# V turned by VectorE instead of TensorE, and seven Strassen products summed in PSUM, in a decoder block on one core

## The chip, the cores and the metric

The kernel runs on one core of a Trainium2 chip. A core has five engines with instruction queues of their own, each served in order: TensorE (PE in the profile, with its weight loads as PEld), VectorE (DVE), ScalarE (ACT), GpSimd (POOL) and SyncE (SP), which issues most of the DMAs. TensorE writes to PSUM, eight banks of 128x512 float32; the other tiles lie in SBUF, and the large intermediates in DRAM. The metric is the device time of one execution in microseconds. Lower is better.

## The reference, cut to what matters

The block has sequence 2048 and width 1024, all in float32. One input projection gives 72 tiles of 128 columns; the tiles are numbered f = 0 to 71 below.

```python
proj = x @ w_in + b_in                        # (2048, 1024) @ (1024, 9216)
q, k, v, g_attn, u_lru, g_lru, gate_logits = split(proj)   # 12, 12, 12, 4, 8, 8, 16 tiles of 128
q, k = rope(q), rope(k)
o_g, lse_g = dilated_band_attention(q_g, k_g, v_g)         # 3 groups of 8 heads, bands of 128 keys
attn = sum_g softmax(lse)_g * o_g
y_a = (attn * silu(g_attn)) @ w_attn_proj
u = causal_depthwise_conv(u_lru);  h = rg_lru(u)           # a scan over positions
y_b = (h * silu(g_lru)) @ w_lru_proj
merged = sigmoid(gate_a) * y_a + sigmoid(gate_b) * y_b
out = layer_norm(alpha * x + merged @ w_out + b_out)
```

V enters the result only through a sum that is linear in it, and that sum is multiplied by silu(g_attn): if a tile of V and the tile of silu(g_attn) beside it both change their sign, nothing changes.

## The kernel before, in words

**Stages.** Stage A computes the input projection with everything that follows it per column tile (rotary, the recurrence, the gates); stage B is the attention; then come the projections of the two branches and the output layer. The change lies in stage A. There the result is held with features on partitions and 512 tokens along the free axis, so that a tile of the projection is 128 features by 512 tokens. The attention wants V with tokens on partitions, so V has to be turned.

**Products.** Every matrix product takes three matmuls of 128x512 per 128 rows of the contraction: each operand is split in a high part (`h`, the rounded copy that ScalarE makes) and a rest (`l`, the difference that VectorE makes), and high times high, high times rest and rest times high are summed. A product of one 128-column tile with half the contraction (512 rows) and 512 tokens is thus 12 matmuls into one PSUM bank.

**Quads.** `plan` lists 72 quads: 36 pairs of column tiles (f0, f1) for the first 1024 tokens, then the same 36 for the second. A quad has four results: two tiles by two token chunks (c0, c1). The first quad of each half is computed plainly with eight products. All others use the Strassen-Winograd scheme with seven products, numbered 1 to 7; `UNIT` names the combination of weights of each (A11, A12, S1 to S4, A22), `BLK` that of x (B11, B21, B22, T1 to T4). The x side is prepared once per half, the weight side for each quad: a weight tile is loaded or summed (S), copied by ScalarE (`h`) and subtracted by VectorE (`l`). For the second half the rests are loaded from DRAM.

**After a product.** The order of the products within a quad is MID (1, 6, 7, 5, 2, 4, 3) for nearly all quads. Each product has a bank of its own from a pool `q` of four, and `evacuate` takes each bank out: ScalarE copies product 1 to SBUF (`e`), VectorE adds product 6 to it (`u`), product 7 to that (`v`), product 5 to `u` again, and four further VectorE instructions (`result`, through `total`) add the last product of each result and its bias. That is seven VectorE instructions and one ScalarE copy for a quad. The results of odd tiles (f1) come out negated. Each result starts a chain (`qk_chain`, `v_chain`, `silu_chain`, `mg_chain`, `lru`): a Python generator whose steps are released by the planner.

**V before.** `v_chain` has TensorE turn the 128x512 result with four transposes (`vtp<-ident,y`, L358) into a bank from a pool `t` of two; ScalarE copies the bank to SBUF (`vs`, L366) and takes the sign back; SyncE stores `vs` to `v_scr` (L370) in pieces of 128 features of a token. There are 12 V tiles and four chunks, so 48 of these.

**What sets the order.** The instruction order of every engine is written out by hand: the main loop runs over `where`, one entry (a tick) per product. In each tick it issues the product, then the events due in this tick (weight loads, copies, splits), then the steps of the chains, then `evacuate`. A chain's step runs when its lag in ticks is over, when its tiles are free, and when the planner's budget of each engine it names (2.75 us per tick, minus what was spent) is not used up; the costs in the `Ask` calls are the planner's. Tiles that a DMA stores are given back two ticks after the issue (`give_sent`); their next writer waits for the DMA to land.

Of the kernel before, what the change touches and what calls it, by code (L numbers as in the profile page):

```python
# [31 lines left out]
def hybrid_block_kernel(ctx: ExitStack, tc: tile.TileContext, a: dict, out: bass.AP):  # L32
# [89 lines left out]
    MID, EDGE, FIRST = (1, 6, 7, 5, 2, 4, 3), (1, 2, 6, 7, 4, 5, 3), (1, 2, 3, 6, 7, 5, 4)  # L122
# [89 lines left out]
    def hi_lo(n, kk, src, eng=dve):  # L212

        t = XB[n][:, kk]
        act.activation(t[:, 0], src, AF.Copy)  # L215
        eng.tensor_tensor(out=t[:, 1], in0=src, in1=flat(t[:, 0]), op=ALU.subtract)
# [47 lines left out]
    def prep_w(s, j):  # L264
# [5 lines left out]
        spend(ACT=.66)  # L270
        if (s, j // 2) not in LO:
            LO[s, j // 2] = take_lo(f"l{j}_{s}")
        l = LO[s, j // 2][1][:, j % 2]
        if plan[s][2] is None or not plan[s][0]:
            tt(dve, l, r, flat(h), ALU.subtract)
            spend(DVE=.71)
        give(r)
        U[s, n] = (h, l)
# [69 lines left out]
    vs_free = [sl_p.tile([P, 4, P], F32, name=f"vs{j}") for j in range(2)]  # L348
    tog = {"n": 0}

    def v_chain(vt, sgn, f, c):
        g, hp = divmod(f - FT_V, 4)
        st = {}

        def turn():
            tp = st["tp"] = ps.tile([P, 4, P], F32, tag="t", name=f"vtp{f}_{c}", bufs=2)
            for b in range(4):
                pe.transpose(tp[:, b, :], flat(vt)[:, b * P:(b + 1) * P], ident)  # L358
# [7 lines left out]
        act.activation(vs, st["tp"], AF.Copy, scale=sgn)  # L366
# [3 lines left out]
        sp.dma_start(dst.rearrange("(b p) f -> p b f", p=P), vs)  # L370
        vs_free.append(vs)
# [26 lines left out]
    def silu_chain(y, sgn, f, c):  # L398
# [3 lines left out]
        act.activation(y, y, AF.Identity, scale=0.25 * sgn, bias=bq[:, f:f + 1])  # L402
# [153 lines left out]
    for h in range(2):  # L556
        for p, (kind, f0, f1) in enumerate(seq):
            plan.append((h, ((f0, kind), (f1, kind)), None if p == 0 else EDGE if p == len(seq) - 1 else FIRST if p == 1 else MID, p, kind))
    NQ = len(plan)
    ticks = [8 if pl[2] is None else 7 for pl in plan]  # L560
    base = [sum(ticks[:s]) for s in range(NQ + 1)]
# [45 lines left out]
    def product(s, j):  # L607
# [4 lines left out]
        else:  # L612
            n, x, first, last, end = UNIT[order[j]], XB[BLK[order[j]]], True, True, True
        if first:
            Q["b"] = ps.tile([P, CH], F32, tag="q", name=f"q{j}_{s}", bufs=4)
        bank = Q["b"]
        h, l = U[s, n]
        i = 0
        for kk in range(4):
            ks = slice(kk * P, (kk + 1) * P)  # L620
            for w, xx in ((h, 0), (h, 1), (l, 0)):
                pe.matmul(bank, w[:, ks], x[:, kk, xx], start=(first and i == 0), stop=(last and i == 11))  # L622
                i += 1
            if i == 6:
                run(pe_late)
        if end:
            del U[s, n]
            give(h)
            u = units_of(s).index(n)
# [3 lines left out]
    def evacuate(s, j):  # L633
        half, _, order, _, _ = plan[s]
        b = Q["b"]
        c0, c1 = 2 * half, 2 * half + 1
        if order is None:
            fi, k, c = PLAIN[j]
            if k:
                result(s, fi, c0 + c, b, None)  # L640
            return
        pid = order[j]
        if pid == 1:
            Q["e"] = take(f"e{s}", F32)
            act.activation(Q["e"], b, AF.Copy)
        elif pid == 2:
            result(s, 0, c0, b, Q["e"])
        elif pid == 6:
            Q["u2"] = take(f"u{s}", F32)
            tt(dve, Q["u2"], Q["e"], b, ALU.subtract)  # L650
        elif pid == 7:
            Q["u3"] = take(f"v{s}", F32)
            tt(dve, Q["u3"], Q["u2"], b, ALU.add)
        elif pid == 5:
            result(s, 1, c1, b, Q["u3"])
# [936 lines left out]
```

## Time and profile before

| | us |
|---|---|
| median of three runs | 2104.55 (2104.39 to 2104.73) |
| span of the profiled execution | 2101.9 |
| TensorE busy in the span | 2086.3 (99%) |
| VectorE busy | 1662.7 (79%) |
| ScalarE busy | 1116.7 (53%) |
| GpSimd busy | 493.1 (23%) |

The span is the time from the first to the last instruction of the profiled execution; the timed runs take some microseconds more than a span. Stage A is the stretch from the start to 1443.7 us, the attention that to about 1643 us. "Busy" of TensorE is the union of its matmuls, which overlap: a matmul listed with 390 ns starts its successor much earlier. What a matmul costs is therefore read from the distances between starts.

### The profile page before, as it was taken

The numbers are of one execution on the slowest core, as the hardware profiler recorded it, in microseconds if no ns is written. First come the engines' busy times: TensorE is split into PE (matmuls) and PEld (weight loads), VectorE is DVE, ScalarE is ACT, GpSimd is POOL, SyncE is SP. The second block draws the span as 40 slices with busy tenths as digits, with TensorE's granted clock in tenths as the row PEclk, the third lists the DMA queues.
The fourth block names the chain that finished last, engine by engine and source line by source line (L and its number), as shares of the span: only waits on it lengthen the run. The fifth ranks groups of instructions, "written<-read, shape, count | busy, mean of one in ns | idle before, by whom it ended". The sixth has DMA issues, their size and how long they took to land.

```text
span 2101.9 us, 35814 instructions
## 1 busy us (share of the span) xinstructions
PE 2086.3 (99%) x12016; PEld 1726.9 (82%) x12016; DVE 1662.7 (79%) x3179; ACT 1116.7 (53%) x2341; POOL 493.1 (23%) x468
## 2 busy tenths in 40 slices
PE   8999999999999999999999999999999999999998
PEld 7888888888888888888888888888999888888887
DVE  8987888889988867787877888877999645576667
ACT  6455456457457565666666775766999411211100
POOL 1111111110111011231221222222545344431120
PEclk9999999999999999999999999999999999999999
DMA  8987997987997967777779778769996788864432
GB/s 271 276 261 225 274 285 216 282 283 235 278 294 242 332 208 204 231 227 220 225 254 278 254 252 266 252 219 374 355 359 236 228 296 281 298 224 160 154 105 71
DMA packets 327160, 524.69 MB, mean 250 GB/s; under 512 B 105536, under 2 KB 135232, under 8 KB 323136
## 3 DMA queue, kind: packets, MB, share of 16 engines
q1 hardware_dynamic: 307088, 489.54, 70.5%
q0 software_dynamic: 12256, 19.42, 5.5%
q10 hardware_dynamic: 7632, 13.44, 1.7%
q8 instruction: 96, 1.57, 0.3%
q14 instruction: 88, 0.72, 0.1%
HBM read 317.14 MB, written 190.45 MB: 241 GB/s over the span
## 4 chain that ended last, share of the span: by engine, by line
PE 91%; DVE 3%; DMA 3%; ACT 2%; issue 1%; SPq 0%; DVEq 0%; ACTq 0%
PE q L622 66%; PE yb L1340 3%; PE yb L1341 3%; PE z L1451 3%; PE yb L1342 3%; PE z L1450 3%; PE z L1452 3%; ACT p L1023 2%; DVE p L1015 2%; PE ya L1419 1%; PE ya L1418 1%; PE ya L1420 1%; PE g L492 1%; PE vtp L358 1%; DMA B<-k_scr 1%; DMA o_scr<-ot 1%
## 5 line engine op out<-in xcount | busy, mean ns | idle before, releaser
L622 PE MATMUL q<-xT,hS 128*128 128x512 f32 x1680 | 521.0, 391 | 0.0
L622 PE MATMUL q<-xT,l 128*128 128x512 f32 x1120 | 436.0, 389 | 0.0
L622 PE MATMUL q<-xB,hA 128*128 128x512 f32 x1248 | 388.9, 393 | 6.0 <-ACT xB L215 6.0
L622 PEld LDWEIGHTS q<-xT,hS 128*128 128x128 f32 x1680 | 312.9, 188 | 69.0 <-issue 5.5
L622 PE MATMUL q<-xB,l 128*128 128x512 f32 x904 | 352.9, 390 | 0.0
L622 PEld LDWEIGHTS q<-xB,hA 128*128 128x128 f32 x1248 | 233.8, 189 | 57.3 <-ACT xB L215 6.0
L622 PEld LDWEIGHTS q<-xT,l 128*128 128x128 f32 x1120 | 210.2, 188 | 44.1
L622 PEld LDWEIGHTS q<-xB,l 128*128 128x128 f32 x904 | 170.3, 188 | 36.0
L245 POOL DMA_DIRECT2D wS<-in_w_in_dram x70 | 61.9, 950 | 491.5 <-DMA wS<-in_w_in_dram 140.0
L622 PE MATMUL q<-xB,hS 128*128 128x512 f32 x560 | 174.0, 392 | 0.0
L1023 ACT ACTIVATE p<-p,sta 128x256 f32<-128x256 f32 (+1 forms) x384 | 172.7, 469 | 1.2 <-PE pt L1034 0.8
L622 PE MATMUL q<-xT,hA 128*128 128x512 f32 x560 | 173.0, 390 | 0.0
L269 ACT ACTIVATE hA<-wA 128x512 fp32r<-128x512 f32 x218 | 134.9, 623 | 54.4 <-DMA wA<-in_w_in_dram 24.9
L269 ACT ACTIVATE hS<-S 128x512 fp32r<-128x512 f32 x175 | 109.0, 623 | 79.3 <-DVE S L227 49.0
L227 POOL TENSOR_TENSOR S<-S,wA 128x512 f32<-128x512 f32 x35 | 45.5, 1301 | 391.8 <-DVE S L227 208.8
L622 PEld LDWEIGHTS q<-xT,hA 128*128 128x128 f32 x560 | 104.7, 188 | 23.0 <-issue 1.5
L622 PEld LDWEIGHTS q<-xB,hS 128*128 128x128 f32 x560 | 104.0, 188 | 22.4 <-issue 1.5
L1015 DVE CUSTOM_DVE_ANT_0 p<-s,mask 128x256 f32<-128x256 f32 (+1 forms) x384 | 116.4, 360 | 0.2 <-PE s L1008 0.2
L1451 PE MATMUL z<-wo,mh 128*128 128x512 f32 (+1 forms) x264 | 101.0, 383 | 0.0
L1452 PE MATMUL z<-wo,ml 128*128 128x512 f32 (+1 forms) x264 | 101.0, 383 | 0.0
L1450 PE MATMUL z<-wo,mh 128*128 128x512 f32 (+1 forms) x264 | 101.0, 383 | 0.0
L227 DVE TENSOR_TENSOR l<-wA,hA 128x512 fp32r<-128x512 f32 x113 | 79.3, 702 | 26.9 <-ACT hA L269 26.6
(204 smaller groups left out, 4257.0 us busy)
## 6 DMA issues: line engine op xcount, KB each, us to landing
wA<-in_w_in_dram SPq DMA_DIRECT2D x253, 256.0 KB, 4.7
wl_scr<-l SPq DMA_DIRECT2D x105, 512.0 KB, 5.2
l<-wl_scr SPq DMA_DIRECT2D x105, 512.0 KB, 4.6
sw<-y SPq DMA_DIRECT2D x384, 64.0 KB, 3.2
wS<-in_w_in_dram SPq DMA_DIRECT2D x70, 256.0 KB, 4.8
wS<-in_w_in_dram POOLq DMA_DIRECT2D x70, 256.0 KB, 6.3
qh_scr<-hi SPq DMA_DIRECT2D x48, 256.0 KB, 5.5
v_scr<-vs SPq DMA_DIRECT2D x48, 256.0 KB, 4.4
```

Of the source, the lines that this page charges most:

```text
L227: eng.tensor_tensor(out=out, in0=in0, in1=in1, op=op)
L245: pool.dma_start(t, w_part(s, x), accum_op=ALU.add)
L269: act.activation(h, r, AF.Copy)
L622: pe.matmul(bank, w[:, ks], x[:, kk, xx], start=(first and i == 0), stop=(last and i == 11))
L1015: dve.tensor_tensor_reduce(out=st["p", i, j][:, h, lo:256], in0=st["s", i, j // 2][h][:, j % 2, lo:256], in1=mask[:, lo:256], scale=1.0, s ...
L1023: act.activation(p, p, AF.Exp, scale=-1.0, bias=s[:, h:h + 1], accum_out=s[:, 2 + h:3 + h])
L1340: pe.matmul(yb, WL[f][:, 0, k], xx[:, 0], start=(k == 0), stop=False)
L1341: pe.matmul(yb, WL[f][:, 0, k], xx[:, 1], start=False, stop=False)
L1342: pe.matmul(yb, WL[f][:, 1, k], xx[:, 0], start=False, stop=(k == 7))
L1450: pe.matmul(z, mh[:, k], w[:, 0, hs], start=(k == 0), stop=False)
L1451: pe.matmul(z, mh[:, k], w[:, 1, hs], start=False, stop=False)
L1452: pe.matmul(z, ml[:, k], w[:, 0, hs], start=False, stop=(k == 7))
```

## The change

Three things change in stage A, all in the code that issues it.

1. **V.** The four transposes, the ScalarE copy and SyncE's store of each V result go. VectorE turns the result in 32x32 blocks within SBUF (one instruction, `vs<-y`, L359 of the new file): the block in partition group a and token group b holds 32 tokens by 32 features afterwards. Four DMAs, one for each group of 32 partitions, put the blocks at their places in `v_scr`; ScalarE issues them, in runs of 32 features (128 bytes). `v_scr` holds the same layout as before. The sign of the odd V tiles is no longer taken back; instead the odd tiles of silu(g_attn) keep their negative sign, by a negated bias.
2. **Sums in PSUM.** Products 1, 6 and 5 go into one bank (A), one after another without clearing; ScalarE copies the bank after each (`e`, `u`, `v`). Products 7 and 4 go into another (C), product 2 into B and product 3 into D. T2 is made with the opposite sign so that product 6 adds. Each result is then one VectorE instruction: B with `e`, C with `v`, D with `v`, and C (after product 4) with `u`. Pool `q` has six banks, pool `t` is gone.
3. **Order.** The products stand as 1, 2, 7, 6, 3, 5, 4, and product 4 is issued four products into the next quad, after its product 6. In the last quad of a half product 4 comes last. The events of the unit that product 4 uses (A22) move with it.

```diff
+    ORDER, LAST = (1, 2, 7, 6, 3, 5, 4), (1, 2, 7, 6, 5, 3, 4)
+    BANK = {1: "A", 2: "B", 6: "A", 7: "C", 5: "A", 3: "D", 4: "C"}
...
+        if n == "T2":
+            act.activation(t[:, 0], src, AF.Copy, scale=-1.0)
+            dve.scalar_tensor_tensor(out=t[:, 1], in0=src, scalar=-1.0, in1=flat(t[:, 0]), op0=ALU.mult, op1=ALU.subtract)
+            return
...
-            for b in range(4):
-                pe.transpose(tp[:, b, :], flat(vt)[:, b * P:(b + 1) * P], ident)
-            give(vt)
-
-        yield Ask(cond=lambda: tog["n"] < 2)
-        tog["n"] += 1
-        pe_later(2, turn)
-        yield Ask(lag=3, cond=lambda: len(vs_free) > 0, ACT=.66)
-        vs = vs_free.pop(0)
-        act.activation(vs, st["tp"], AF.Copy, scale=sgn)
-        tog["n"] -= 1
-        yield Ask()
-        dst = v_scr[g][hp // 2][c * CH:(c + 1) * CH, (hp % 2) * P:(hp % 2) * P + P]
-        sp.dma_start(dst.rearrange("(b p) f -> p b f", p=P), vs)
-        vs_free.append(vs)
+        yield Ask(need=1, DVE=.72)
+        vs = take(f"vs{f}_{c}", F32)
+        dve.transpose(vs, flat(vt))
+        give(vt)
+        yield Ask(lag=2, ACT=1.4)
+        dst = v_scr[g][hp // 2][c * CH:(c + 1) * CH].rearrange("(b i) f -> i b f", i=32)
+        for a in range(4):
+            f0 = (hp % 2) * P + 32 * a
+            act.dma_start(dst[:, :, f0:f0 + 32], vs[32 * a:32 * a + 32].rearrange("p (b f) -> p b f", f=32))
+        give_sent(vs)
...
+        js = list(range(8 if pl[3] == 0 else 7 if pl[3] == len(seq) - 1 else 6))
+        own = [(s, j) for j in js]
+        where += own[:4] + ([(s - 1, 6)] if pl[3] > 1 else []) + own[4:]
...
+            n, x, last, end = UNIT[order[j]], XB[BLK[order[j]]], True, True
+            first = order[j] in (1, 2, 7, 3)
+        b = s, BANK[order[j]] if order else "P"
         if first:
-            Q["b"] = ps.tile([P, CH], F32, tag="q", name=f"q{j}_{s}", bufs=4)
+            Q[b] = ps.tile([P, CH], F32, tag="q", name=f"q{j}_{s}", bufs=6)
...
+        if pid in (1, 6, 5):
+            n = {1: "e", 6: "u", 5: "v"}[pid]
+            Q[s, n] = take(f"{n}{s}", F32)
+            act.activation(Q[s, n], b, AF.Copy)
         elif pid == 2:
-            result(s, 0, c0, b, Q["e"])
+            result(s, 0, c0, b, Q[s, "e"])
+            give(Q.pop((s, "e")))
-        elif pid == 6:
-            tt(dve, Q["u2"], Q["e"], b, ALU.subtract)
-        elif pid == 7:
-            tt(dve, Q["u3"], Q["u2"], b, ALU.add)
-        elif pid == 5:
-            result(s, 1, c1, b, Q["u3"])
-            tt(dve, Q["u2"], Q["u2"], b, ALU.add)
...
+    def between(s, j):
+        b = order.index(5)
+        if j == b:
+            result(s, 1, 2 * plan[s][0] + 1, Q[s, "C"], Q[s, "v"])
+        if j == max(b, order.index(3)):
+            result(s, 0, 2 * plan[s][0] + 1, Q[s, "D"], Q[s, "v"])
+            give(Q.pop((s, "v")))
...
+        if T:
+            between(*where[T - 1])
```

`between` runs in the tick after product 5, so the results that need `v` are issued one product after the copy.

**TensorE, at a V quad.** The names are q(place in the quad)_(quad): `q0_5` is the bank of product 1 of quad 5. Before, the four transposes of a V result stand in the middle of a product:

```order
L358 MATMUL vtp25_1_1244<-ident_180,y25_1_1181 128x128 x4
L622 MATMUL q6_4_1237<-xB22_365,hS4_4_1153 128x512 x2
L622 MATMUL q6_4_1237<-xB22_365,l6_4_1155 128x512
...
L622 MATMUL q0_5_1265<-xB11_272,hA11_5_1176 128x512 x2
L622 MATMUL q0_5_1265<-xB11_272,l0_5_1178 128x512
...
L358 MATMUL vtp24_0_1272<-ident_180,y24_0_1211 128x128 x4
```

Now no transposes stand there, product 6 goes into product 1's bank (`q0_6`), product 4 of quad 5 into the bank of its product 7 (`q2_5`) in the middle of quad 6, then product 3 (`q4_6`) and product 5, again into `q0_6`:

```order
L625 MATMUL q0_6_1415<-xT2_425,hS2_6_1400 128x512 x2
L625 MATMUL q0_6_1415<-xT2_425,l2_6_1373 128x512
...
L625 MATMUL q2_5_1275<-xT4_582,hA22_5_1396 128x512 x2
L625 MATMUL q2_5_1275<-xT4_582,l6_5_1398 128x512
...
L625 MATMUL q4_6_1556<-xB22_362,hS4_6_1428 128x512 x2
L625 MATMUL q4_6_1556<-xB22_362,l4_6_1430 128x512
...
L625 MATMUL q0_6_1415<-xT1_524,hS1_6_1453 128x512 x2
L625 MATMUL q0_6_1415<-xT1_524,l4_6_1430 128x512
```

So between two products of bank A stand two others, in which ScalarE's copy of the bank has to be done.

**ScalarE, at the V quads 10 and 11.** Before, one copy `e` and the copies `vs` of the turned V stand among the copies of weights (hA, hS):

```order
L335 ACTIVATE hi_1_2277<-y_1_1977 128x512
L269 ACTIVATE hA_10_2301<-wA_10_2107 128x512
L366 ACTIVATE vs_219<-vtp_1_2257 128x512
L645 ACTIVATE e_2314<-q_10_2283 128x512
L269 ACTIVATE hA_10_2329<-wA_10_2212 128x512
L335 ACTIVATE hi_0_2333<-y_0_2055 128x512
L366 ACTIVATE vs_220<-vtp_0_2290 128x512
L269 ACTIVATE hS_10_2360<-S_10_2189 128x512
L269 ACTIVATE hA_11_2392<-wA_11_2271 128x512
L366 ACTIVATE vs_219<-vtp_0_2349 128x512
```

Now `v` and `e` stand there, and the stores in groups of four:

```order
L365 DMA v_scr_77<-vs_0_2301 32x16x32 x4
L342 ACTIVATE hi_0_2352<-y_0_2134 128x512
L274 ACTIVATE hA_10_2371<-wA_10_2263 128x512
L274 ACTIVATE hS_11_2375<-S_11_2265 128x512
L649 ACTIVATE v_2387<-q_10_2195 128x512
L274 ACTIVATE hS_11_2402<-S_11_2290 128x512
L365 DMA v_scr_77<-vs_1_2355 32x16x32 x4
L365 DMA v_scr_77<-vs_1_2357 32x16x32 x4
L649 ACTIVATE e_2424<-q_11_2389 128x512
L274 ACTIVATE hS_11_2439<-wS_11_2123 128x512
L365 DMA v_scr_77<-vs_0_2422 32x16x32 x4
```

Two groups stand back to back right ahead of an `e` here; such a pair stands at eleven places of stage A.

**VectorE, at a V quad.** Before, three sums out of PSUM (`u`, `v`, `u`) stand between the results:

```order
L227 TENSOR_TENSOR u_2547<-e_2520,q_11_2522 128x512
L227 TENSOR_TENSOR l_11_2564<-S_11_2390,hS_11_2562 128x512
L227 TENSOR_TENSOR S_12_2566<-wS_12_2420,wA_12_2475 128x512
L227 TENSOR_TENSOR y_0_2457<-y_0_2457,cos_637 128x512
L227 TENSOR_TENSOR sw_0_2484<-sw_0_2484,sin_638 128x512
L227 TENSOR_TENSOR v_2571<-u_2547,q_11_2549 128x512
L227 TENSOR_TENSOR S_12_2586<-S_12_2566,wA_12_2508 128x512
L227 TENSOR_TENSOR l_12_2590<-wA_12_2475,hA_12_2588 128x512
L568 SCALAR_TENSOR_TENSOR y_1_2593<-q_11_2573,bn,v_2571 128x512
L227 TENSOR_TENSOR u_2547<-u_2547,q_11_2573 128x512
```

Now two results with `v` stand together, and the two turned tiles follow:

```order
L567 SCALAR_TENSOR_TENSOR y_1_1811<-q_7_1669,bn,v_1790 128x512
L567 SCALAR_TENSOR_TENSOR y_1_1813<-q_7_1735,b_193,v_1790 128x512
L232 TENSOR_TENSOR l_8_1807<-wS_8_1548,hS_8_1830 128x512
L232 TENSOR_TENSOR gw_0_1835<-gr_202,gw_0_1835 128x128
L359 STREAM_TRANSPOSE vs_1_1838<-y_1_1811 128x512
L359 STREAM_TRANSPOSE vs_1_1840<-y_1_1813 128x512
```

The three sums are gone from VectorE's queue, and one instruction per V result has come.

More of the change, by code (lines that the diff above doesn't have):

```diff
@@ L270, in prep_w @@
         spend(ACT=.66)
+        U[s, n] = h
+        if plan[s][2] is not None and plan[s][0]:
+            give(r)
+            return
         if (s, j // 2) not in LO:
@@ L612, in product @@
         else:
-            n, x, first, last, end = UNIT[order[j]], XB[BLK[order[j]]], True, True, True
+            n, x, last, end = UNIT[order[j]], XB[BLK[order[j]]], True, True
+            first = order[j] in (1, 2, 7, 3)
+        b = s, BANK[order[j]] if order else "P"
         if first:
-            Q["b"] = ps.tile([P, CH], F32, tag="q", name=f"q{j}_{s}", bufs=4)
-        bank = Q["b"]
-        h, l = U[s, n]
+            Q[b] = ps.tile([P, CH], F32, tag="q", name=f"q{j}_{s}", bufs=6)
+        bank = Q[b]
+        h = U[s, n]
+        u = units_of(s).index(n)
+        l = LO[s, u // 2][1][:, u % 2]
         i = 0
@@ L621, in product @@
             for w, xx in ((h, 0), (h, 1), (l, 0)):
-                pe.matmul(bank, w[:, ks], x[:, kk, xx], start=(first and i == 0), stop=(last and i == 11))
+                pe.matmul(bank, w[:, ks], x[:, kk, xx], start=(first and i == 0), stop=(last and i == 11),
+                          skip_group_check=not first and order is not None)
                 i += 1
@@ L628, in product @@
             give(h)
-            u = units_of(s).index(n)
             if u % 2 or u == 6:
@@ L925, in hybrid_block_kernel @@
     low = NS
-    where = [(s, j) for s in range(NQ) for j in range(ticks[s])]
     for T, (s, j) in enumerate(where):
```

68 lines of the change are left out of this document (25 added, 43 removed).

## The prediction

> **What bounds the kernel now.** I read the page first: the span, TensorE's share, its row in forty slices, the granted clock and the chain that ended last.
>
> ```profile
> span 2101.9 us, 35814 instructions
> PE 2086.3 (99%) x12016; PEld 1726.9 (82%) x12016; DVE 1662.7 (79%) x3179; ACT 1116.7 (53%) x2341; POOL 493.1 (23%) x468
> ...
> PE   8999999999999999999999999999999999999998
> ...
> PEclk9999999999999999999999999999999999999999
> ...
> q1 hardware_dynamic: 307088, 489.54, 70.5%
> ...
> PE 91%; DVE 3%; DMA 3%; ACT 2%; issue 1%; SPq 0%; DVEq 0%; ACTq 0%
> ```
>
> TensorE sets the end, at full clock. The change lies in stage A, so next comes the table by stretches (columns: length, then busy time of PE, PEld, DVE, ACT, POOL, clock, DMA share, GB/s).
>
> ```profile
> 100.00:1100.00 1000.00, 1000.00 (x4529) 817.22 (x4528) 827.74 (x1248) 572.30 (x940) 165.40 (x172) 1.00 0.82 251
> 1100.00:1443.00 343.00, 343.00 (x1526) 278.89 (x1525) 268.05 (x374) 227.15 (x361) 80.50 (x65) 1.00 0.82 261
> ```
>
> In stage A TensorE has no hole at all, while VectorE is at 83% and ScalarE at 57% of the first stretch. So a TensorE instruction that goes is worth its full pitch, a VectorE instruction that goes is worth nothing by itself, and anything that makes TensorE wait costs its full length.
>
> **Term 1, the transposes that go.** All 48 lie in stage A, four to a V result; the timeline of TensorE around one group gives their pitch.
>
> ```profile
> L358 PE MATMUL vtp<-ident,y 128*128 128x128 f32 x192 | 28.5, 272 | 0.0
> ```
>
> ```profile
> 1086.23 0.39 PE L622 MATMUL q<-xB,l 128*128 128x512 f32 x1
> 1086.46 0.60 PE L358 MATMUL vtp<-ident,y 128*128 128x128 f32 x4
> 1086.82 0.71 PE L622 MATMUL q<-xB,hS 128*128 128x512 f32 x2
> 1087.37 0.40 PE L622 MATMUL q<-xB,l 128*128 128x512 f32 x1
> 1087.60 0.62 PE L622 MATMUL q<-xB,hS 128*128 128x512 f32 x2
> 1088.06 0.39 PE L622 MATMUL q<-xB,l 128*128 128x512 f32 x1
> ```
>
> From one `l` matmul to the next, with three matmuls, it is 1088.06 - 1087.37 = 0.69 us; with a group of four transposes between it is 1087.37 - 1086.23 = 1.14 us. So a group costs 0.45 us, and 48 x 0.45 = 21.6 us go. (The busy time of 28.5 us counts overlap and is not what they cost.) The number of 128x512 matmuls stays: seven products of twelve. Summing in PSUM needs no extra one.
>
> **What VectorE gains and pays.** It loses three sums a quad and gets one turn per V result.
>
> ```profile
> L227 DVE TENSOR_TENSOR u<-e,q 128x512 f32<-128x512 f32 x70 | 47.7, 682 | 27.2 <-PE q L622 27.1
> L227 DVE TENSOR_TENSOR v<-u,q 128x512 f32<-128x512 f32 x70 | 47.7, 681 | 25.1 <-PE q L622 25.0
> L227 DVE TENSOR_TENSOR u<-u,q 128x512 f32<-128x512 f32 x70 | 47.4, 676 | 0.0
> L227 DVE TENSOR_TENSOR rp<-y,sw 128x512 f32<-128x512 f32 x64 | 74.3, 1166 | 0.4
> ```
>
> The turn stands in no row. It moves 128x512 float32 like the sums (0.68 us); the dearest row of that size, the regrouping `rp`, has 1.17 us. I take 0.7. Then 47.7 + 47.7 + 47.4 = 143 us leave and 48 x 0.7 = 34 us (at most 56) come. Worth on the path: nothing, since TensorE was not waiting for VectorE. It is cover for what follows.
>
> **What ScalarE pays.** Two more copies out of PSUM in each of 70 quads, 48 copies `vs` fewer, and 192 DMA issues.
>
> ```profile
> L645 ACT ACTIVATE e<-q 128x512 f32<-128x512 f32 x70 | 41.1, 588 | 93.3 <-PE q L622 84.6 <-POOL sw L227 6.4 <-DMA mg_scr<-y 2.2
> L366 ACT ACTIVATE vs<-vtp 128x512 f32<-128x512 f32 x48 | 27.6, 589 | 30.4 <-DMA v_scr<-vs 14.1 <-PE vtp L358 12.4 <-PE q L622 3.9
> ```
>
> Copies: 140 x 0.59 - 48 x 0.59 = +54 us. An issue of 32 partitions in sixteen pieces of 128 bytes is in no row. The nearest ones, by line (minimum, median and maximum in ns), are the old V store, one ScalarE store, the rotary halves (32 partitions each), and a pair of stores with pieces of 128 bytes, `qh` and right behind it `ql`:
>
> ```profile
> L370 SPq DMA_DIRECT2D v_scr<-vs x48: 365/384/1181, 106.6 to 1105.0; - x48
> L386 ACTq DMA_DIRECT2D mg_scr<-y x5: 326/326/327, 1426.3 to 1445.3; - x5
> L307 SPq DMA_DIRECT2D sw<-y x384: 507/588/1542, 61.5 to 1390.1; - x192
> L341 SPq DMA_DIRECT2D qh_scr<-hi x16: 524/577/1058, 77.1 to 1293.7; - x16
> L341 SPq DMA_DIRECT2D ql_scr<-rp x16: 2115/2678/5558, 77.8 to 1294.4; - x16
> 847.31 2.42 SPq L307 DMA_DIRECT2D sw<-y  x4
> ```
>
> A group of four costs ScalarE's queue between 4 x 0.326 = 1.3 us and, if each of the later three waits as `ql` does, 0.58 + 3 x 2.68 = 8.6 us. I take 2.4 us: the last row is four issues of 32 partitions in a row, and `ql` per piece agrees (it waits behind 2048 pieces; a quarter of 2.68 is 0.67, and 0.58 + 3 x 0.67 = 2.6). So 48 x 2.4 = 115 us come, and ScalarE goes from 572 to about 720 us in the first stretch: busy, not full.
>
> **Term 2, ScalarE's copies are now in TensorE's way.** Product 6 may not start before `e` has left bank A, product 5 not before `u`, and the next C not long after `v`. Between stand two products of 4 x 0.68 = 2.72 us, so a copy may end 5.4 us after its product. How late ScalarE is today shows at its worst in the timeline: product 1 ends where product 6 starts (first row), and `e` comes 5.2 us later.
>
> ```profile
> 568.75 0.62 PE L622 MATMUL q<-xT,hS 128*128 128x512 f32 x2
> ...
> 573.97 0.58 ACT L645 ACTIVATE e<-q 128x512 f32<-128x512 f32 x1
> ```
>
> ```profile
> ACT e L645 <- PE q L622: 84.6, 27, 7.2
> ACT hi L335 <- DVE rp L227: 36.3, 14, 8.1
> ```
>
> At 27 of 70 copies ScalarE was early and waited. Late ones come from ScalarE standing behind VectorE (second row, up to 8.1 us), which gets rarer with an emptier VectorE. The eleven pairs of groups are the new strain: the pair stands in the tick of the copied product, so it has three products, 8.2 us, for 2 x 2.42 + 0.59 = 5.4 us, and 2.7 us of lateness fit. If the second group also waits as `ql` does (2.1 us more), 0.6 us fit; say seven of eleven are 2 us late, then 7 x 1.4, about 10 us, are lost. Below, nothing. I take 2.5 us, near the row of four issues.
>
> **Term 3, the first Strassen quad.** Here both engines are late from the start.
>
> ```profile
> 11.48 0.62 PE L622 MATMUL q<-xB,hA 128*128 128x512 f32 x2
> ```
>
> ```profile
> 40.32 2.49 DVE L227 TENSOR_TENSOR xcB<-xcB,xcB 128x512 f32<-128x512 f32 x4
> ```
>
> ```profile
> 41.04 2.44 ACT L215 ACTIVATE xT<-xcB 128x512 fp32r<-128x512 f32 x4 [2.26 <-DVE xcB L227]
> ```
>
> `u` now stands behind these four T4 copies and one weight copy. One more weight sum ahead of the `xcB` differences, and T2's dearer form, move them by about 1 us, so T4 ends at 44.5 and `u` at 45.5. Product 5 is the fourteenth; the second starts at 11.48, so it is due at 11.48 + 12 x 2.72 = 44.1. I book 1.3 us, between 0 and 3. T3, needed two products earlier than today, is still in time.
>
> **Term 4, the end of stage A.** Product 4 is now last and leaves its bank by one VectorE sum (0.68 us); the attention's first scores may want that bank. 0 to 1 us; I take 0.5.
>
> **V's stores.** SyncE loses 48 issues, which nobody waited for. Nobody reads `v_scr` before the end of stage A, but a tile is given back two ticks after the issue. Stores of 128-byte pieces land a little later than the old V stores (L341, then L370):
>
> ```profile
> DMA to landing us min/median/max: 4.2/5.7/11.1
> ```
>
> ```profile
> DMA to landing us min/median/max: 2.3/4.4/7.7
> ```
>
> The 32 stores of L341 go by with TensorE full, so I book nothing. The Trainium skill ("DMA: Bandwidth & Descriptors", Specifications) speaks against the change: it asks for at least 512 bytes, since a smaller transfer is read, modified and written. By the rows here the landing agrees with a loss, of 1.3 us each, off the path; by the rule alone the DMA engines would be the bound, which is the last rival.
>
> **Sum.** 2101.9 - 21.6 + 2.5 + 1.3 + 0.5 = 2084.6 us of span. The timed median lies 2104.55 - 2101.9 = 2.65 us above the span, so **2087 us**.
>
> **Rivals.**
> - *ScalarE is late more often.* For it: 43 of 70 copies `e` were late already, and there are three times as many. Against it: ScalarE keeps a quarter free. With ten waits of 1 us at `u` and `v` and half of the pairs' 10 us, 15 us go: 2104.55 - 21.6 + 1.8 + 15 = 2100 at the edge, typically 2097.
> - *The waits eat the whole gain*, the pairs' 10 us and ten waits of 1 us together: 2104.55 - 21.6 + 1.8 + 20 = 2105, no change.
> - *The issues fill ScalarE* (slower). A V quad and the one behind it last 2 x 19.5 = 39 us; ScalarE's other work there is 2 x 11.2 us (572 us over 51 quads), copies gone and come cancel, so four groups have 16.6 us, 4.15 us each. Beyond that TensorE waits 48 us for each further microsecond; the gain is gone at 4.6 us. At the longest `ql` wait for a whole group, 5.56 us: 48 x 1.41 = 68 us, 2151 us. For it speaks the `ql` row, against it that a group has as many pieces as one `qh`, which goes in 0.58 us.
> - *The DMA engines fill up* (slower). A packet of the SyncE queue takes 0.705 x 16 x 2101.9 / 307088 = 77 ns on average. The V pieces rise from 24576 to 98304. If time goes by packets, 73728 x 77 ns / 16 = 355 us come on a stretch that has 180 us free; if by bytes, none. It decides from 39 ns per packet; at 45 ns it costs 27 us, 2112 us. Against it: L341's landings.
>
> That the transposes stay is no rival: none is left in TensorE's order.
>
> **Chances and range.** The forecast (2080 to 2095) 0.60, the first rival 0.17, no change 0.09, ScalarE full 0.10, DMA full 0.04. A measurement of this kernel can tell about 0.2% (4.2 us) from no change. Faster is forecast and first rival, 0.77; same 0.09; slower 0.14. The range, 2079 to 2106, takes in the first rival and no change, leaves out the slower ones, and below allows the transposes' pitch and no stall at all.
>
> **What would show it.** Right: stage A ends near 1426 us with TensorE's busy time equal to its length; `e`, `u`, `v` show as releasers of TensorE with a few microseconds in all; a group of stores takes about 2.4 us on ScalarE's queue; the turn about 0.7 us. Wrong: TensorE idle before products 6 or 5 in every V quad, or groups above 4 us, or matmuls with a longer pitch when they add to a bank.

## The result, and the profile after

The changed kernel takes 2184.99 us (median of 4 runs, 2180.95 to 2186.90) against 2104.57 us before: 1.0378 times, 95% interval 1.0363 to 1.0392. It is slower by 80 us, where 17 us less were forecast.

The page of the changed kernel: TensorE's busy time, its row in forty slices, the granted clock, ScalarE's DMA queue, the landing of V's stores, and the costliest group of TensorE with its idle time.

```profile
span 2182.6 us, 35099 instructions
PE 2093.8 (96%) x11824; PEld 1720.6 (79%) x11824; DVE 1598.4 (73%) x3018; ACT 1159.0 (53%) x2431; POOL 502.9 (23%) x468
...
PE   8999799799999999998898999998999999999998
...
PEclk9999899999999999999999999999999999999999
...
q10 hardware_dynamic: 109008, 26.04, 5.5%
...
L625 PE MATMUL q<-xT,hS 128*128 128x512 f32 x1680 | 534.0, 400 | 59.8 <-ACT e L649 52.8
...
v_scr<-vs ACTq DMA_DIRECT2D x192, 64.0 KB, 4.3
```

The stretches of stage A, which now ends 80 us later (columns as in the prediction):

```profile
100.00:1100.00 1000.00, 945.67 (x4100) 764.47 (x4099) 742.66 (x1090) 563.16 (x942) 157.18 (x160) 0.98 0.83 238
1100.00:1524.00 424.00, 405.92 (x1771) 326.67 (x1771) 296.11 (x383) 277.71 (x450) 105.33 (x83) 0.98 0.79 249
```

TensorE, which had no hole in these stretches, has 72 us of them, and its clock is no longer full. VectorE is emptier (74% of the first stretch), ScalarE computes less than before (56%), the DMA engines' share is where it was. No engine is busy all the time. What TensorE waits for (total, times, longest):

```profile
PE q L625 <- ACT e L649: 52.8, 16, 11.8
PE q L625 <- DMA l<-wl_scr: 8.1, 2, 7.9
PE q L625 <- ACT xB L220: 5.9, 1, 5.9
PE q L625 <- ACT u L649: 4.1, 3, 2.9
```

The third row is the start, as before. The first is the copy of product 1 out of bank A, to which product 6 adds. In the second, `l` is a rest of the weights that SP loads from DRAM, called a low half below.

**All of it is in stage A.** In the trace the last product ends at 1443.8 us before and 1523.8 us after; the rest of the program takes 658.1 and 658.7 us. The transposes' 21.6 us are gone, so 80 + 21.6 = 102 us were lost. Two pieces hold some 98 of them. From the starts of successive matmuls, 23 waits over 0.5 us make 76.5 us. And the matmuls after a wait come slowly: 111 further ones stand over 0.38 us apart instead of 0.227, 24 us more in all, against 11 of them and 3 us before. The costliest place, on TensorE:

```profile
237.54 0.39 PE L625 MATMUL q<-xT,l 128*128 128x512 f32 x1
249.73 1.22 PE L625 MATMUL q<-xT,hS 128*128 128x512 f32 x2 [11.80 <-ACT e L649]
250.75 0.63 PE L625 MATMUL q<-xT,l 128*128 128x512 f32 x1
251.18 1.05 PE L625 MATMUL q<-xT,hS 128*128 128x512 f32 x2
```

and the same time on ScalarE, where ACTq is its queue issuing DMAs:

```profile
230.07 3.52 ACTq L365 DMA_DIRECT2D v_scr<-vs  x4
233.69 0.63 ACT L342 ACTIVATE hi<-y 128x512 fp32r<-128x512 f32 x1 [2.99 <-DMA v_scr<-vs]
...
235.27 0.57 ACT L649 ACTIVATE v<-q 128x512 f32<-128x512 f32 x1
235.75 0.62 ACT L274 ACTIVATE hS<-S 128x512 fp32r<-128x512 f32 x1
235.78 13.18 ACTq L365 DMA_DIRECT2D v_scr<-vs  x8
249.08 0.60 ACT L649 ACTIVATE e<-q 128x512 f32<-128x512 f32 x1 [12.72 <-DMA sw<-y]
```

A pair of store groups holds ScalarE's queue for 13.2 us, `e` stands behind it, and TensorE behind `e`. ScalarE also came to the pair late: the product that `e` copies had ended at about 232.3, but another group and five operations of ScalarE stood ahead of the pair, so when the pair began at 235.78 TensorE had work for only 2.2 us more. The issues themselves are short:

```profile
L365 ACTq DMA_DIRECT2D v_scr<-vs x192: 309/439/1738, 97.7 to 1193.7; - x192
```

Summed over the trace, the 192 issues last 105 us, 2.2 us a group. From the first issue's start to the last one's end a group takes 4.2 us on average and up to 9.3; the ten pairs that nothing interrupts take 6.1 to 13.8 us. The difference is time between issues of one group. The instruction order of the changed kernel shows what stands there (the listing of ScalarE with the semaphores each row waits for):

```
L365 DMA v_scr_77<-vs_1_2355 32x16x32 [waits DMAHW3_49,DVE_49]
L365 DMA v_scr_77<-vs_1_2355 32x16x32 [waits DMAHW6_49]
L365 DMA v_scr_77<-vs_1_2355 32x16x32 [waits DMAHW7_49]
L365 DMA v_scr_77<-vs_1_2355 32x16x32 [waits DMAHW0_49]
L365 DMA v_scr_77<-vs_1_2357 32x16x32 [waits DMAHW3_49,DVE_49]
L365 DMA v_scr_77<-vs_1_2357 32x16x32 [waits DMAHW6_49]
L365 DMA v_scr_77<-vs_1_2357 32x16x32 [waits DMAHW1_49]
L365 DMA v_scr_77<-vs_1_2357 32x16x32 [waits DMAHW4_49]
L649 ACTIVATE e_2424<-q_11_2389 128x512 [waits DMAHW2_49,PE_49,Pool_49]
```

These are the eight issues of that place. DMAHW0 to 7 are eight completion semaphores, given out in turn over the DMAs of SP and ScalarE together. An issue waits until the earlier transfer with its semaphore has landed. Read from the trace, each issue beside that transfer (us):

```
issue starts   earlier transfer on its semaphore   issued by, at     it landed
235.78         v_scr<-vs                           ScalarE 230.96    235.70
237.37         v_scr<-vs                           ScalarE 232.18    237.35
242.30         wl_scr<-l                           SP      234.67    242.28
242.88         qh_scr<-hi                          SP      235.60    242.86
244.50         v_scr<-vs                           ScalarE 235.78    244.42
245.77         v_scr<-vs                           ScalarE 237.37    244.97
247.57         k_scr<-rp                           SP      243.51    247.55
248.62         sw<-y                               SP      245.33    248.60
```

Seven of the eight start within 0.1 us after a landing; the sixth starts when the fifth has ended. The third waited 4.6 us for a write of low halves, the seventh for a K store that SP itself issued only at 243.51. Over the whole trace 55 issues of V's stores start within 0.25 us of such a landing after more than 0.3 us of idling, 95 us together; 41 of them and 69 us were for transfers of SP. These 55 start 0.02 us after the landing, and none of the 192 starts ahead of it. So ScalarE's queue had become tied to SP's. What the Trainium skill says ("Perfetto Trace Analysis", DMA Instruction — HWDGE (DVE, Sync)) agrees: the start that the profile reports for such a DMA is the moment at which all its semaphores are satisfied.

### The profile page after: what moved, and what is told of

The parts are those of the page before. It is cut to its first block, busy times and chain, and to the rows that moved or that the text cites. A ratio compares the mean times of both kernels' runs of the same rounds, so it can differ in the third digit from the quotient of the medians.

```text
span 2182.6 us, 35099 instructions
## 1 busy us (share of the span) xinstructions
PE 2093.8 (96%) x11824; PEld 1720.6 (79%) x11824; DVE 1598.4 (73%) x3018; ACT 1159.0 (53%) x2431; POOL 502.9 (23%) x468
## 5 line engine op out<-in xcount | busy, mean ns | idle before, releaser
L625 PE MATMUL q<-xT,hS 128*128 128x512 f32 x1680 | 534.0, 400 | 59.8 <-ACT e L649 52.8
L625 PE MATMUL q<-xT,l 128*128 128x512 f32 x1120 | 444.1, 397 | 8.1 <-DMA l<-wl_scr 8.1
L625 PEld LDWEIGHTS q<-xT,hS 128*128 128x128 f32 x1680 | 320.8, 193 | 138.8 <-ACT e L649 60.6
L625 PEld LDWEIGHTS q<-xT,l 128*128 128x128 f32 x1120 | 215.3, 192 | 55.1 <-DMA l<-wl_scr 9.0
L232 POOL TENSOR_TENSOR S<-S,wA 128x512 f32<-128x512 f32 x35 | 55.2, 1578 | 365.5 <-DVE S L232 253.6
L649 ACT ACTIVATE u<-q 128x512 f32<-128x512 f32 x70 | 41.2, 588 | 114.6 <-PE q L625 64.2
L232 DVE TENSOR_TENSOR y<-y,cos 128x512 f32<-128x512 f32 x96 | 89.0, 929 | 17.0 <-DMA sw<-y 17.0
L1451 PE MATMUL z<-wo,mh 128*128 128x512 f32 (+1 forms) x264 | 101.0, 383 | 0.0
```

What stands on the lines that cost most here:

```text
L232: eng.tensor_tensor(out=out, in0=in0, in1=in1, op=op)
L1451: pe.matmul(z, mh[:, k], w[:, 1, hs], start=False, stop=False)
```

## The experiments

Where the stores change their engine or their number (e1, e3, e9 and the runs built on them), what the planner charges an engine for them changes too (the `Ask` of `v_chain`), so a few other steps may have shifted as well. Four theories stood at the start. *ScalarE*: store issues hold its queue, the copies behind them are late. *Small pieces*: 128-byte pieces slow the DMA engines. *Sums*: copies out of shared banks with 5.4 us of slack are too late by themselves. *Slots*: tiles come back late behind the stores.

### Who issues the stores, and how many

**e1_sp**, SP instead of ScalarE:

```diff
-            act.dma_start(dst[:, :, f0:f0 + 32], ...)
+            sp.dma_start(dst[:, :, f0:f0 + 32], ...)
```

> The changed kernel with its 192 V stores issued by SP instead of ScalarE; nothing else differs. ScalarE theory (the groups of four store issues hold ScalarE's queue, the copies e, u, v stand behind them, TensorE waits): the 52.8 us of waits for e fall under 10 us, stage A ends near 1430 us and the time is 2080 to 2100 us, with some us lost if SP's loads come late behind 192 more issues. Small-piece theory (the 128-byte pieces slow the DMA engines): the pieces are the same, so 2170 to 2190 us. Sums theory (three copies out of shared banks with 5.4 us of slack are too late by themselves): 2170 to 2190 us. Slot theory (tiles given back after the stores come back late, and the copies wait for tiles): SP's stores land no earlier, 2170 us or more.

Measured: 2133.55 us, 1.0137 times the kernel before (1.0120 to 1.0154). 51 us come back with the bytes and pieces unchanged: the ScalarE theory's direction, but 34 us above the upper end of its range. The waits of TensorE:

```profile
PE q L625 <- DMA l<-wl_scr: 13.2, 5, 8.1
PE q L625 <- ACT e L649: 12.3, 7, 4.1
```

At the two largest waits for `e` that are left (4.0 us each) it stands behind two SiLU operations on ScalarE, which wait for VectorE's sums; low halves that SP loads came late five times.

**e3_one_store** and **e3b_four_long**, ScalarE with one store, or four, in pieces of 512 bytes. Both leave out putting the blocks at their places: V's rows lie in the wrong order in `v_scr`, and the work of the engines is the same.

```diff
-        for a in range(4): ...
-            act.dma_start(dst[:, :, f0:f0 + 32], vs[32 * a:32 * a + 32] ...)
+        act.dma_start(dst.rearrange("(b p) f -> p b f", p=P), vs ...)          # e3_one_store
+        for b in range(4): act.dma_start(dst[:, b, :], vs[:, b * P:(b + 1) * P])   # e3b_four_long
```

> The changed kernel with one store per V result on ScalarE (48 issues instead of 192, the same bytes in pieces of 512 instead of 128 bytes). V's rows land in the wrong order, so attention works on a wrong V; the work of every engine is the same. ScalarE theory: 2080 to 2100 us, the wait for e under 10 us. Small-piece theory: also 2080 to 2100 us. Sums theory: 2170 to 2190 us.

> The changed kernel with four stores per V result on ScalarE as it has them (192 issues), but each in 128 pieces of 512 bytes instead of 512 pieces of 128 bytes. V's rows land in the wrong order, so attention works on a wrong V. ScalarE theory, if the number of issues is what costs: still 2160 to 2190 us. Small-piece theory: 2080 to 2100 us. Sums theory: 2170 to 2190 us.

Measured: 2120.40 us (1.0060 to 1.0090 times) and 2141.36 us (1.0156 to 1.0186). Both lie outside every range named; both theories were half right. Four issues instead of one cost 21 us; pieces of 128 instead of 512 bytes, with as many issues, another 44 us (each store of e3b also reads 128 partitions instead of 32; the two were not separated). The waits for landings on ScalarE, counted as above, follow: 0.4 us, 22.7 us, and 95 us in the changed kernel. By these rows the piece size acts through the landing, which releases the next issue:

```profile
v_scr<-vs ACTq DMA_DIRECT2D x192, 64.0 KB, 3.3
```

against 4.3 us with 128-byte pieces.

**e9_pool**, POOL instead of ScalarE. By the trace POOL's transfers use eight other semaphores, and none of its 192 issues starts at a landing after a wait.

```diff
-            act.dma_start(dst[:, :, f0:f0 + 32], ...)
+            pool.dma_start(dst[:, :, f0:f0 + 32], ...)
```

> The changed kernel with its stores issued by POOL and nothing else changed. Shared-semaphore theory: the waits for e fall from 52.8 to about 12 us, as they did with SP and with one store; the last load's 8 us stay; 2110 to 2130 us. If POOL is filled by the stores, S units come late: 2135 us or more.

Measured: 2126.27 us, 1.0102 times (1.0087 to 1.0117), as the theory had it. Pieces of 128 bytes, and no tile back sooner (landing 4.8 us), yet the waits for `e` are 11.2 us: neither the DMA engines nor the slots held the changed kernel. POOL's price for an issue is small:

```profile
L365 POOL DMA_DIRECT2D v_scr<-vs x192: 648/651/1313, 96.9 to 1116.2; - x192
```

### Place in the queue, or length of the hold

**e2_copies_first**:

```diff
+        if early_copy:            # products 1, 6 and 5
+            evacuate(s, j)
         run(late)
         run_chains()
 ...
-        evacuate(s, j)
+        if not early_copy: evacuate(s, j)
```

> The changed kernel with one thing moved: in each tick the copies e, u and v are issued on ScalarE ahead of whatever the chains issue in that tick (store groups, silu, h copies of chains), not behind it. The stores stay on ScalarE, four per V result. Place-in-the-queue theory (a copy is late because store groups of its own tick, and silu's two operations waiting for VectorE's sums, stand ahead of it): the waits for e fall from 52.8 us to under 15 us and the time is 2105 to 2130 us. Held-for-long theory (groups and pairs of groups hold ScalarE longer than the two or three products until the next copy, wherever they stand): waits for u and v grow in place of e, 2140 to 2170 us. Sums theory: 2175 to 2190 us.

Measured: 2185.26 us, 1.0385 times (1.0367 to 1.0402): nothing gained. The waits only moved:

```profile
PE q L625 <- ACT u L649: 34.7, 9, 10.4
PE q L625 <- DMA l<-wl_scr: 13.5, 4, 10.6
PE q L625 <- ACT e L649: 10.7, 7, 3.5
```

`e` is mostly in time, and `u`, the next copy, is behind the stores. The hold is longer than the time from one copy to the next. My place-in-the-queue theory fell. The time lies above the range of the held-for-long theory too, and in that of the sums theory, which e1 and e9 rule out: they keep the sums and lose most of these waits.

**e11_spread**, the four issues in four ticks:

```diff
-        yield Ask(lag=2, ACT=1.4)
         for a in range(4):
+            yield Ask(lag=1 if a else 2, ACT=.35)
             act.dma_start(...)
```

> The changed kernel with the four stores of a V result issued by ScalarE in four ticks, one each, not together in one; nothing else changes, and the copies stand where they stood. Held-queue theory (each issue waits for the landing of the transfer that had its semaphore, and what hurts is that four or eight such waits follow one another ahead of a copy): ScalarE's waits for landings stay of the order of 95 us in all, but a copy has one of them ahead of it, so the waits for e fall from 52.8 to 15 to 30 us, 2130 to 2160 us. If what hurts is the sum of the waits wherever they stand: 2175 us or more. If it were the stores' bytes and pieces alone: 2175 us or more too.

Measured: 2144.33 us, 1.0189 times (1.0175 to 1.0203): 41 us back with the same issues, bytes and pieces. TensorE waits 12.3 us for `e` and 14.2 us for `u`. The waits for landings on ScalarE fell too, to 61 us, so the gain may come from fewer waits as well as from fewer of them in a row ahead of one copy. How it divides was not separated.

### The parts alone

**e4_new_sums_old_turn**, the sums in PSUM with V turned by TensorE as before (into the gates' two banks, with ScalarE's one copy and SP's one store):

> The changed kernel's sums in PSUM with V turned as before: four TensorE transposes per V result into the two banks of the gates, one ScalarE copy, one SP store of 512-byte pieces. Sums theory: the waits for e, u and v stay, 2165 to 2200 us (the transposes' 21.6 us come back on top). ScalarE and small-piece theories: no stalls over 5 us, 2100 to 2115 us: the transposes' 21.6 us are back, so about the kernel before.

Measured: 2124.37 us, 1.0096 times (1.0081 to 1.0111). The stalls at `e` and `u` are nearly gone, which the sums theory (2165 us or more) did not allow, but it is not the kernel before, and 9 us above the range of the two others:

```profile
PE q L636 <- DMA l<-wl_scr: 8.3, 2, 8.1
PE q L636 <- ACT u L660: 2.4, 3, 1.0
PE q L636 <- DVE y L232: 2.2, 1, 2.2
```

A row like the first, 6.6 to 10.6 us at the longest, is in every run with the new sums that keeps this load where the change put it. The change loads the last quad's seventh low half four products later, since in other quads that product moved by five; in the last quad it moved by one.

**e6_load_early** takes this back in the changed kernel, **e10_sums_load_early** in e4:

```diff
-at(t0 + j - 1 + (4 if j == 6 else 0), ...load_lo...)
+at(t0 + j - 1 + (4 if j == 6 and plan[s][3] < len(seq) - 1 else 0), ...load_lo...)
```

> The changed kernel with the load of the last quad's seventh low half issued four products earlier (as far ahead of its product as the kernel before had it). In the trace of the change and of all four runs so far TensorE waits 8 us for this load at the end of the first stage. Late-load theory: that wait goes and 8 to 11 us with it, 2173 to 2178 us. If the wait is only taken over by another one behind it (the last copies, or the stage after it): under 3 us, 2182 us or more.

> The sums in PSUM with V's old turn (e4, 2124.4 us) and the last low half loaded four products earlier. Terms that add: 8.2 us of waiting and about 2.5 us of slow matmuls go, 2112 to 2116 us; the new sums would then cost about 9 us over the kernel before by their stalls at e, u and the change of halves. If that load only hides another wait: 2119 us or more.

Measured: 2174.62 us (1.0320 to 1.0351 times), 10 us back as expected; and 2120.21 us (1.0063 to 1.0094), 4 us back instead of 8 to 12, as was expected if the load only hides another wait. In e10 the last product ends 5 us sooner, but the attention's first scores then wait:

```profile
1458.79 1.83 PE L1019 MATMUL s<-B,A 64*128 64x128 f32 x24
1465.90 3.37 PE L1019 MATMUL s<-B,A 64*128 64x256 f32 x24 [5.29 <-DVE sta L1026]
```

Why VectorE is late there in e10 and not in e6 is open, and so is whether the other three executions have this wait: they took 2118 to 2122 us, the one with the profile 2125.

**e5_old_sums_new_turn**, **e5b_old_sums_sp** and **e5p_old_sums_pool**: the kernel before with V's new turn alone, stored by ScalarE, SP or POOL.

```diff
-    NS, NL = 32, 4
+    NS, NL = 34, 4          # in the place of the two tiles vs_free
+        dve.transpose(vs, flat(vt))
+            act.dma_start(...)      # e5; sp in e5b, pool in e5p
```

> The kernel before with V's new turn alone: VectorE turns it, ScalarE issues four stores of 128-byte pieces; the products are summed as before, in four banks, with one or two copies per quad on ScalarE; two more slots in the place of the two tiles that V had. ScalarE theory: a copy has three products' time (8.2 us) before its bank is used again, so a group of 4 us mostly hides and a pair of 8 to 13 us does not: 2085 to 2110 us with a few stalls of 1 to 5 us behind the copies. Sums theory (the new turn costs nothing): 2081 to 2086 us, no stalls. Small-piece theory: stalls on loads, 2130 us or more.

> The kernel before with V's new turn alone, as in e5, its four stores per V result issued by SP. Shared-semaphore theory (an issue on ScalarE or SP waits until the transfer that had the same one of eight completion semaphores has landed; in the change 55 issues on ScalarE started within 0.25 us of such a landing, after 95 us of waiting together): ScalarE's 91 us of such waits in e5 go, SP takes 192 issues and waits itself, so e5's 2137.4 falls to 2085 to 2105 us; what is left is low halves that SP loads late. If SP is what is full: 2110 us or more.

> The kernel before with V's new turn alone, its four stores per V result issued by POOL, whose transfers go through a software queue. Shared-semaphore theory: neither ScalarE nor SP waits for these stores: 2083 to 2095 us. If POOL's own cost for a store of 512 pieces is over 2 us, 192 of them (400 us and more beside its 500 us) make its sums of weights late: stalls on S units, 2100 us or more.

Measured: 2137.42 us (1.0147 to 1.0179 times), 2119.03 us (1.0052 to 1.0086), 2099.81 us (0.9969 to 0.9987). So ScalarE's stores hurt without the new sums as well, and 27 us more than the upper end expected. They reach TensorE by other ways too: the weight copies `hA` and `hS` stand behind them, VectorE's rests `l` wait for those (87 us instead of 43 before), and then the old sums are late.

```profile
ACT hA L269 <- DMA v_scr<-vs: 52.2, 8, 9.7
ACT hS L269 <- DMA v_scr<-vs: 34.9, 9, 6.7
...
PE q L610 <- ACT e L633: 10.1, 2, 9.1
PE q L610 <- DVE v L227: 9.9, 5, 3.6
PE q L610 <- DVE y L556: 8.8, 3, 7.0
```

With SP (e5b) the time lies where it was expected if SP is what is full, and TensorE waits 10.3 us for low halves. With POOL the kernel is faster than before, yet 5 of 21.6 us is little. Its stretches by halves of stage A (e5p, then the kernel before):

```profile
0.00:717.00 717.00, 699.83 (x3075) 568.24 (x3076) 632.07 (x1015) 373.90 (x617) 160.61 (x223) 1.00 0.90 265
717.00:1442.00 725.00, 720.75 (x3197) 585.22 (x3196) 584.46 (x823) 454.57 (x731) 227.05 (x234) 1.00 0.81 246
```

```profile
0.00:717.00 717.00, 711.03 (x3184) 582.43 (x3185) 618.50 (x994) 389.02 (x645) 97.63 (x127) 1.00 0.88 267
717.00:1444.00 727.00, 727.00 (x3280) 591.62 (x3278) 566.31 (x796) 463.32 (x751) 164.08 (x137) 1.00 0.78 244
```

In the first half VectorE is busy for 632 us instead of 619 and the DMA share is 0.90 instead of 0.88; TensorE has 11 us more holes, as much as 24 groups of transposes cost there (10.8 us). Which of the two is short there was not separated.

### Together

**e7_sp_first_load** and **e12_pool_first_load**: the changed kernel with the stores on SP or POOL, the copies first and the load early. **e13_half**: the kernel before, with e5p's turn in the second half alone.

> The changed kernel with three things together: V's stores on SP, the copies ahead of the chains' work in each tick, and the last low half loaded four products earlier. If the three causes add up (e1 measured 2133.6 with 12.3 us of waits for e, of which silu's operations stood ahead, and 13.2 us of waits for low halves, 8.1 of them the last): 2133.6 less 12 to 16 us for the copies with their slow matmuls, less 8 to 11 us for the load: 2105 to 2115 us. If SP is what is full, the low halves of the second half come later still: 2115 to 2130 us. Below 2095 us only if the slow matmuls after stalls vanish as well.

> The changed kernel with its stores on POOL, the copies ahead of the chains' work in each tick, and the last low half loaded four products earlier: all that the runs have shown to cost, taken away together. e9 (POOL alone) 2126.3 less 7 us for the load, less 2 to 3 us of slow matmuls, less 4 to 8 of its 11 us of waits for e: 2106 to 2114 us. If the copies' place only shifts the wait from e to u, as in e2: 2114 to 2119 us.

> The kernel before with V's new turn (VectorE, POOL's stores) in the second half alone; in the first half V is turned by TensorE as before, through a slot in the place of a tile of its own. In e5p, which has the new turn in both halves, progress counted by the copies of the weights stood 3 us behind the kernel before at the end of the first half and 5 us ahead of that at the end of the second. If the halves are independent: 2096 to 2100 us, at least as fast as e5p's 2099.8. If the second half's gain needs what the first half's new turn leaves (VectorE and SP's queue): 2100 to 2104 us.

Measured: 2124.37 us (1.0077 to 1.0110 times), 2118.38 us (1.0048 to 1.0075) and 2095.10 us (0.9944 to 0.9971). The first two stay 9 and 4 us above the sums of their parts: e7 where it was expected if SP is what is full, e12 where it was expected if the copies' place only shifts a wait (TensorE waits 8.1 us for `u` in it, and 5.4 us for low halves). With all known causes taken away the changed kernel still takes 14 us more than the kernel before. The new sums bring that along: with V's old turn and the early load (e10) they take 16 us more. The third beats both kernels; TensorE waits for next to nothing in stage A:

```profile
PE q L633 <- ACT xB L215: 5.5, 1, 5.5
PE q L633 <- DMA l<-wl_scr: 1.8, 2, 1.6
PE q L633 <- ACT hA L269: 0.5, 1, 0.5
```

Its stage A ends 8.5 us sooner than before, 0.5 of it by the first row, at the start. 24 x 0.45 = 10.8 us of transposes went.

## Why the prediction was wrong

- **Term 1, right.** A group of transposes is worth 0.45 us: e13 gains 8.0 us of 10.8 behind its start and shows 2.3 us of what is missing as waits (1.8 and 0.5). In the changed kernel the gain came, and 102 us were lost against it.
- **The turn, right.** 0.7 us was taken:

```profile
L359 DVE STREAM_TRANSPOSE vs<-y x48: 664/704/712, 95.9 to 1169.3; 128x512 f32<-128x512 f32 x48
```

- **What ScalarE pays: the step that failed.** The group of four stores was taken as 2.4 us. The issuing alone was that (2.2 us), but a group holds the queue for 4.2 us, a pair for 6.1 to 13.8 us instead of 4.8. The price was read from SP's rows, `sw` four in a row, and these could hardly show it: the 96 such groups of the kernel before take 2.40 to 3.86 us, and only four of their issues waited for a landing (2.5 us). In all of its stage A SP has 23 such waits, 19 us; in the changed kernel SP has 46, 33 us. What stands ahead of a copy was asked of ScalarE's work, never of the semaphores on which its new instructions wait, though they stand in the instruction order. The sign that the prediction had named for this, groups above 4 us, showed.
- **Term 2, booked at 2.5 us with 10 as its end, was 57 us of waits** (`e` 52.8, `u` 4.1). Both sides of its comparison failed. The pair's time with the copy, 5.4 us, was the price above. And a pair does not have 8.2 us: that holds if ScalarE reaches it when the copied product starts. ScalarE reached the four pairs that stand ahead of an `e` with 8.1, 6.5, 3.0 and 2.2 us left before TensorE stood, and TensorE waited 5.4, 4.9, 11.6 and 11.8 us there, 34 of the 57. With the booked 5.4 us the last two would still have cost some 6 us (an estimate: 5.4 - 3.0 and 5.4 - 2.2). The first two rivals named these waits, with 15 and 20 us.
- **The rival "the issues fill ScalarE" named the place and not the mechanism.** It asked for a sustained 4.15 us per group before anything is lost, and 4.6 us before the gain is gone. With the mean, 4.2 us, it gives a loss of 2 to 3 us; ScalarE computes for 56% of the first stretch. What decides is how long single holds are against the time to the next copy. (Its 2151 us leaves out the 1.8 us of terms 3 and 4 that the other rivals carry; with them it is 2152.)
- **Nothing was booked for the landing of V's stores, and that was wrong**, and with it the reading that longer landings lie off the path. The Trainium skill's rule of at least 512 bytes ("DMA: Bandwidth & Descriptors", Specifications) was right in direction, through a way not thought of: 44 us between e3b and the changed kernel. The rival "the DMA engines fill up" fell: a share of 0.83 against 0.82, and e9 with the same pieces is 59 us faster.
- **Term 3** (1.3 us) was 1.0 us at 44.9 us in the trace. **Term 4** looked at the bank and not at the last low half, moved by the change: 8 us of waiting and 10 us of time (e6).
- **Nothing was booked for a TensorE that has stood still**: 21 us of slow matmuls.

Of the 80 us, the runs account for 59 us by ScalarE's issues (e9) and 10 us by the last load (e6); with both away and the copies first the kernel stands 14 us above the one before (e12). That remainder (in e12 TensorE waits for late `u`, low halves, `e` and VectorE) was not taken apart further and stays open; e10, with the old turn and 16 us, points to the sums and their order.

## What to carry to other kernels

Before moving a DMA to a compute engine's queue, read the semaphores that its issue waits for: such an engine is held until an older transfer lands, perhaps one of another engine's queue, and whatever stands behind it has to stand that long. Compare the longest such hold, not the mean, with the slack of the next instruction that TensorE needs, and count this slack from the moment at which the engine's queue really gets there. And when work moves by a number of steps, check the last round by itself.

## What the runs showed of the hardware

**TensorE runs at half speed after many of its waits.** Two tables by stretches of the changed kernel; the granted clock is the third number from the end. Before the 11.8 us wait and right after it:

```profile
230.00:237.00 7.00, 7.00 (x32) 5.79 (x32) 6.41 (x12) 3.31 (x6) 3.89 (x6) 1.00 0.97 241
...
249.70:254.00 4.30, 4.27 (x10) 3.40 (x11) 2.58 (x4) 0.50 (x1) 0.00 (x0) 0.50 0.89 196
```

After a wait of 2.9 us, and after one of 1.6 us:

```profile
125.40:129.00 3.60, 3.60 (x9) 2.84 (x10) 3.09 (x5) 3.52 (x6) 3.54 (x6) 0.53 0.91 122
...
158.80:162.00 3.20, 3.15 (x14) 2.58 (x15) 3.12 (x6) 1.72 (x4) 0.00 (x0) 1.00 1.01 349
```

After the waits of 11.8 and 2.9 us matmuls come 0.43 us apart for 5.7 and 3.4 us, then 0.23 again; after 1.6 us they did not. In between, length alone does not decide in this trace: the waits of 2.2 us (to 1088.2) and 2.6 us (to 1152.0) were followed by the slow pitch, those of 2.6 us (to 605.0) and 2.5 us (to 1075.5) were not, nor was one of 3.5 us in e2 (to 1151.1). The 4.3 us of the second row hold ten matmuls, which take 2.3 us at full speed; over the waits of this trace that were followed by it, the slow pitch costs 1.4 to 2.7 us on top of a wait. At the start of the kernel before, 15 matmuls take 6.1 us beside a clock of 1.00, so the pitch tells it more surely than that column. The Trainium skill states this ("TensorE: Matmul & The Clock Gate", Part 1: The HAM clock gate): half rate after an idle window of about 3.4 us, full rate after as long a busy one. The trace agrees on both rates; some of the waits that sufficed here, 2.2 and 2.6 us, were shorter than that.

**Stores from a third queue.** An issue of 512 pieces of 128 bytes costs POOL 0.65 us, without waiting for SP's or ScalarE's transfers, and it was the cheapest place for V's stores (e5p against e5 and e5b: 2099.8, 2137.4 and 2119.0 us).
